# The down product placed behind the next expert's gate and up products, and the odd layer's stepped attention groups stored by residue

## The chip, the cores and the metric

The kernel runs on one core of a Trainium2 chip. The metric is device time in microseconds (us) of one execution of the whole program. The program is a static list of instructions for each engine: TensorE (PE; its weight loads are the row PEld), VectorE (DVE), ScalarE (ACT), GpSimd (POOL) and SyncE (SP), which issues most of the DMA transfers. Each engine works its own list in order and waits on semaphores for the others.

## The reference, cut to what matters

Three blocks follow one another on 512 tokens of width 1024. The first ends in a mixture of 16 experts, in which each expert takes the 64 tokens of highest affinity; the third holds an attention over three groups of keys, of which two are spaced.

```python
aff = softmax(h @ w_router)                # 512 tokens x 16 experts
g, idx = top_k(aff.T, 64)                  # each expert takes its 64 tokens
xin = h[idx]                               # 16 x 64 x 1024
a = xin @ w_gate[e];  u = xin @ w_up[e]    # weights 1024 x 1024 fp32 each
y = (silu(a) * u) @ w_down[e]
y = y * g                                  # then added back to the rows idx
...
DIL_CONFIGS = ((128, 1), (512, 4), (2048, 16))   # window and step of the three groups
# odd layer, one group: a query sees keys 0, dil, 2*dil, ... behind it
s = q @ k[:, local].T * scale - slope * steps;  s[not valid] = -inf
o = softmax over the three groups together, times v
```

## The kernel before, in words

**Weights.** All weights lie in device memory in the order in which they are used, in chunks of [128, 2048] fp32 (1 MB). `fetch` (L372) issues one transfer for a chunk from SP into a ring of buffers; in the expert stage the ring has seven buffers (two of the pool `wp`, five of `pc`), and a transfer waits until the chunk that had its buffer has been used. `pieces` takes a chunk as two pieces of [128, 1024] and writes each as a sum of two reduced-precision parts: ACT copies the high part (`whi`), DVE subtracts it and keeps the rest (`wlo`). PE multiplies with both. Piece 5 of each product (`WHOLE`) is not split: PE takes it from the raw chunk in full fp32, so that chunk's buffer comes free when PE has used it.

**Expert stage (`phase_b`).** Every engine call of the stage but POOL's and SP's is pinned to program order, through a wrapper, so that ACT, DVE and PE run the stage in the order of the Python code; in the profile nearly all of it carries the wrapper's line, L279, and tiles tell the operations apart. One product (`prod`) is eight pieces, "slots 0 to 7"; at each slot the code first draws the next pieces (`piece`, which keeps up to `ahead` pieces converted beyond the one in use, 2 at first and 5 after the first down product has opened the pool `pm`), then runs the side work that is hung on this slot (`hooks`), then issues the slot's matmuls.

`_moe_order` writes out the order of the products: gate and up of expert 0; then gate of e+1, down of e, up of e+1; at the end gate 15, up 15, down 14, down 15.

The side work consists of generators that are advanced one step at a time:

- `gather(e)`: an indirect DMA of the expert's 64 rows from POOL into `xn`, then two steps that transpose them on PE into a bank named `tp` and split them into `xs` (ACT high part, DVE rest); the second also copies one block in full fp32 to `xfull`.
- `activ(e)`: two steps, each of 16 matmul instructions on the gate result `ag` and the up result `xn`, then ACT's SiLU, DVE's product `sg`, and the split into `act`. The first step uses two `tp` banks, the second two `av` banks; there are two of each.
- `pair(p, n)`: the finished rows `yt` of two experts are scaled by DVE, a selection matrix `ph` is made, and the rows are split into `y`; n is 1 (all 1024 columns at once) but for the last pair.
- `scatter`: PE adds the rows of one or two pairs back by a matmul with `ph` into an `av` bank, DVE adds the bank to `x`; eight steps for each group of `GROUPS`.

After an up product ACT copies the result to `xn` (`first`); after a down product ACT copies halves to `ya` and DVE adds them into `yt` (`down`).

**Odd layer (`phase_e`).** `qk` makes `qz` and `kT` of a pair of heads (tokens along the free axis) by projecting, then copying from the result bank. `far` forms the scores of the two spaced groups for four residues c:

```python
nc.tensor.matmul(ps[:, sl], qz[:, t, c::4], kT[:, c::4], start=True, stop=True)
```

Both operands are read with a step of four fp32 elements. In this phase the framework orders instructions itself.

Of the kernel before, what the change touches and what calls it, by code (L numbers as in the profile page):

```python
# [52 lines left out]


def _moe_order():
    o = [("g", 0), ("u", 0)]
    for e in range(NE):
        if e + 1 < NE:
            o.append(("g", e + 1))
        o.append(("d", e))  # L60
        if e + 1 < NE:
            o.append(("u", e + 1))
    o[-3:] = [o[-2], o[-3], o[-1]]
    return o


# [225 lines left out]
class Kernel:  # L292
# [737 lines left out]
    def phase_b(self, er, ep, after):  # L1030
# [72 lines left out]
        def gather(e):  # L1103

            xg = self.nrm.tile([128, D], F32, name="xn", tag="xn")
            nc.gpsimd.indirect_dma_start(out=xg[:CAP], out_offset=None, in_=self.hd[:, :],
                                         in_offset=bass.IndirectOffsetOnAxis(ap=idxg[:, e:e + 1], axis=0))
            yield
            st = pw.tile([128, 8, 128], F32R, name="xs")
            xs[e] = st, xfull[:, e % 2]  # L1110
            for g in range(2):
                pt = self.tp()
                for k in range(4):
                    kk = 4 * g + k
                    nc.tensor.transpose(pt[:, k * CAP:(k + 1) * CAP], xg[:CAP, kk * 128:(kk + 1) * 128],
                                        self.ident[:CAP, :CAP])
                t = pt[:, :4 * CAP].rearrange("p (k c) -> p k c", k=4)
                self.split(st[:, 4 * g:4 * g + 4, :CAP], st[:, 4 * g:4 * g + 4, CAP:], t)
                for n, k in enumerate(WHOLE):
                    if k // 4 == g:  # L1120
                        nc.scalar.copy(xfull[:, e % 2, n, :CAP], t[:, k % 4])
                yield

        def prod(stat, full, hooks):
# [30 lines left out]
        def activ(e):  # L1155
            a = [asb.pop((t, e)) for t in "gu"]
            last = e + 1 == NE
            st = pw.tile([128, 8, 128], F32R, name="act", tag="xs" if last else "act", bufs=2 if last else 1)
            full = xfull[:, NE % 2] if last else afull
            act[e] = st, full  # L1160
            for g in range(2):
                pg, pu = (self.av(), self.av()) if g else (self.tp(), self.tp())
                for src, pt in zip(a, (pg, pu)):
                    for k in range(4):
                        f = 4 * g + k
                        nc.tensor.matmul(pt[:, k * 128:(k + 1) * 128], src[:, f * 128:(f + 1) * 128], dup,
                                         start=True, stop=True)
# [31 lines left out]

        iota = None  # L1200

        def pair(p, n):

            t = rows.pop(p)
            y = pm.tile([128, 2, D], F32R, name="y", bufs=3)
            ph = pm.tile([128, S], F32R, name="ph", bufs=3)
            ys[p] = y, ph
            for i in range(n):
                sl = slice(i * D // n, (i + 1) * D // n)
                nc.vector.scalar_tensor_tensor(t[:, sl], t[:, sl], gp[:, p:p + 1], self.g2[:, sl], op0=OP.mult, op1=OP.mult)  # L1210
                if i == 0:
                    nc.vector.tensor_scalar(ph, iota, idxp[:, p:p + 1], None, op0=OP.is_equal)
                    yield
                self.split(y[:, 0, sl], y[:, 1, sl], t[:, sl])
            yield

        def scatter(ps_, c):

# [19 lines left out]
        gath, acts = gather(0), none  # L1238
        for _ in range(3):
            next(gath)  # L1240
        scat = fin = none
        for t, e in order:
            if t == "g":
                gath = gather(e + 1) if e + 1 < NE else none
                first(t, e, {0: [gath], 2: [acts], 3: [acts], 5: [scat], 7: [scat]})
            elif t == "u":
                fresh = fin is not none
                first(t, e, {1: [fin], 2: [gath], 3: [none if fresh else scat], 4: [gath], 5: [fin],
                             7: [none if fresh else scat]})
                fin = none  # L1250
                acts = activ(e)
            else:
                down(e, {2: [acts], 3: [acts], 4: [scat], 5: [scat], 6: [scat], 7: [scat]} if e + 2 == NE else {})
                if e % 2:
                    p = e // 2
                    fin = pair(p, 2 if e + 1 == NE else 1)
                    if p in GROUPS:
                        list(scat)
                        scat = scatters(GROUPS[p]) if e + 1 < NE else none
        list(fin)  # L1260
        self.nc = nc = plain
        self.parts = []
        el.close()
# [260 lines left out]
    def phase_e(self, hT, after):  # L1524
        nc, tc, sp = self.nc, self.tc, self.sp
        with ExitStack() as es:
# [25 lines left out]
            def qk(scale=1.0):  # L1552
                qz = p.tile([128, 2, S], F32, name="qz", bufs=3)
                nc.gpsimd.memset(qz[64:, 0], 0.0)
                nc.gpsimd.memset(qz[:64, 1], 0.0)
                kT = p.tile([128, S], F32, name="kT", bufs=3)
                for t, w in enumerate(self.pieces("qk", 128)):
                    ps = self.mm()
                    self.proj_s(hT, w, ps)
                    if t == 0:  # L1560
                        nc.scalar.activation(qz[:64, 0], ps[:64], AF.Copy, scale=scale)
                        nc.vector.tensor_scalar(qz[64:, 1], ps[64:], scale, None, op0=OP.mult)
                    else:
                        nc.scalar.copy(kT, ps)
                return qz, kT

            def stick(pr):
# [56 lines left out]
            def dilated(pr):  # L1624
# [20 lines left out]
                def far(g, db, qz, kT):  # L1645
                    for t in range(2):
                        ps = self.mm()
                        for c in range(4):
                            sl = slice(c * 128, (c + 1) * 128)
                            nc.tensor.matmul(ps[:, sl], qz[:, t, c::4], kT[:, c::4], start=True, stop=True)  # L1650
                        for c in range(4):
                            sl = slice(c * 128, (c + 1) * 128)
                            nc.vector.tensor_tensor_reduce(s12[g - 1][t][:, c], ps[:, sl], db[:, t], 1.0, NEG,
# [204 lines left out]
```

## Time and profile before

| | us |
|---|---|
| median of 3 runs (2100.42 to 2102.78) | 2101.84 |
| the profiled execution, its own time | 2099.54 |
| span of the profiled execution | 2097.8 |

The span is what the trace covers; 1.7 us of the execution lie around it. The median of the runs is 2.3 us above the profiled execution's own time. Sums are made against the profiled execution.

The expert stage runs from about 280 to 826 us of the span, the odd layer from about 1480 to 1690 us.

### The profile page before, as it was taken

How to read it: one execution, taken by the hardware profiler on the slowest of the kernel's cores; microseconds unless marked ns; L12 is line 12 of the kernel's file. 1: busy time of each engine (PE TensorE's matmuls, PEld its weight loads, DVE VectorE, ACT ScalarE, POOL GpSimd, SP SyncE). 2: the span in 40 equal slices, each digit the busy share in tenths (PEclk: the TensorE clock that was granted, in tenths of full speed). 3: DMA queues.
4: the chain of work that ended last, by engine and by line, in shares of the span. 5: the costliest groups of instructions: out<-in, count | busy, mean ns of one | idle time of the engine just before them, and what ended most of it. 6: DMA issues, size and time to landing. Idle time of an engine off the chain costs nothing.

```text
span 2097.8 us, 24799 instructions
## 1 busy us (share of the span) xinstructions
PE 1966.8 (94%) x9203; PEld 1554.2 (74%) x9203; DVE 1362.1 (65%) x2286; ACT 1060.8 (51%) x1835; POOL 153.3 (7%) x146
## 2 busy tenths in 40 slices
PE   5889869999999998999989999999999989999998
PEld 5667746767677676877778888888887768888886
DVE  7776478898988888627766533554537676534653
ACT  3335358777777876436544433443325554423432
POOL 2003500000000001000110000001100010000001
PEclk9889979999999999999999999999999999999999
DMA  7653648998999995220123222221421023222221
GB/s 292 195 170 125 285 175 338 366 384 354 405 383 366 389 396 209 91 91 11 61 81 108 94 91 101 101 88 64 133 71 61 33 79 121 96 96 100 81 96 56
DMA packets 53933, 358.30 MB, mean 171 GB/s; under 512 B 6694, under 2 KB 7262, under 8 KB 14004
## 3 DMA queue, kind: packets, MB, share of 16 engines
q1 hardware_dynamic: 48148, 338.60, 42.5%
q0 software_dynamic: 5664, 18.12, 3.2%
q8 instruction: 72, 1.18, 0.2%
q14 instruction: 49, 0.40, 0.1%
HBM read 353.28 MB, written 4.46 MB: 171 GB/s over the span
## 4 chain that ended last, share of the span: by engine, by line
PE 76%; DVE 10%; issue 6%; ACT 5%; DMA 3%; POOL 0%; SPq 0%; ACTq 0%; DVEq 0%; POOLq 0%
PE mm L279 13%; PE mm L411 13%; PE mm L412 13%; PE mm L413 13%; DVE wlo L279 3%; PE av L279 2%; PE av L413 2%; PE av L412 2%; PE av L411 2%; PE tp L411 2%; PE tp L413 2%; ACT whi L279 2%; PE tp L412 2%; DMA wraw<-in_wts 2%; PE mm L1289 1%
## 5 line engine op out<-in xcount | busy, mean ns | idle before, releaser
L402 DVE TENSOR_TENSOR wlo<-wraw,whi 128x1024 fp32r<-128x1024 f32 (+2 forms) x209 | 250.6, 1201 | 412.2 <-ACT whi L401 412.1
L279 DVE TENSOR_TENSOR wlo<-wraw,whi 128x1024 fp32r<-128x1024 f32 x336 | 393.9, 1219 | 46.1 <-ACT whi L279 44.3
L401 ACT CAST whi<-wraw 128x1024 fp32r<-128x1024 f32 (+2 forms) x209 | 214.8, 1030 | 356.5 <-PE mm L412 145.3
L411 PE MATMUL mm<-hT_hi,whi 128*128 128x512 f32 (+1 forms) x960 | 375.3, 392 | 5.1 <-ACT whi L401 4.9
L412 PE MATMUL mm<-hT_lo,whi 128*128 128x512 f32 (+1 forms) x960 | 374.1, 390 | 0.4 <-DVE hT_lo L417 0.4
L413 PE MATMUL mm<-hT_hi,wlo 128*128 128x512 f32 (+1 forms) x960 | 373.8, 390 | 0.0
L279 ACT CAST whi<-wraw 128x1024 fp32r<-128x1024 f32 x336 | 333.1, 1050 | 15.8 <-PE mm L279 14.8
L411 PEld LDWEIGHTS mm<-hT_hi,whi 128*128 128x128 f32 x960 | 182.3, 190 | 46.3 <-ACT whi L401 5.7
L412 PEld LDWEIGHTS mm<-hT_lo,whi 128*128 128x128 f32 x960 | 182.3, 190 | 41.2 <-DVE hT_lo L417 1.6
L413 PEld LDWEIGHTS mm<-hT_hi,wlo 128*128 128x128 f32 x960 | 182.3, 190 | 39.8
L279 PE MATMUL mm<-whi,xs 128*128 128x512 f32 x448 | 199.7, 446 | 2.3 <-ACT whi L279 2.3
L279 PE MATMUL mm<-wlo,xs 128*128 128x512 f32 x448 | 183.1, 409 | 4.0 <-DVE wlo L279 3.7
L279 PEld LDWEIGHTS mm<-wlo,xs 128*128 128x128 f32 x448 | 86.6, 193 | 36.5 <-DVE wlo L279 14.5
L412 PE MATMUL mm<-wlo,hT_hi 128*128 128x512 f32 (+2 forms) x288 | 110.8, 385 | 1.1 <-DVE wlo L402 1.1
L411 PE MATMUL mm<-whi,hT_hi 128*128 128x512 f32 (+2 forms) x288 | 110.9, 387 | 0.0
L413 PE MATMUL mm<-whi,hT_lo 128*128 128x512 f32 (+2 forms) x288 | 110.2, 384 | 0.6 <-DVE hT_lo L417 0.6
L279 PEld LDWEIGHTS mm<-whi,xs 128*128 128x128 f32 x448 | 86.8, 194 | 27.3 <-issue 6.2
L279 PE MATMUL mm<-whi,act 128*128 128x512 f32 x224 | 94.4, 422 | 0.0
L279 PE MATMUL mm<-wlo,act 128*128 128x512 f32 x224 | 89.3, 399 | 0.5 <-DVE wlo L279 0.5
L416 ACT CAST aT_hi<-cv 128x512 fp32r<-128x512 f32 x44 | 27.3, 621 | 117.0 <-DVE cv L1767 117.0
L1766 ACT ACTIVATE cv<-cv 128x512 f32<-128x512 f32 x44 | 27.8, 632 | 89.2 <-DVE cv L1763 89.2
L411 PE MATMUL tp<-whi,aT_hi 128*128 128x512 f32 x176 | 69.4, 395 | 0.0
(502 smaller groups left out, 3382.5 us busy)
## 6 DMA issues: line engine op xcount, KB each, us to landing
wraw<-in_wts SPq DMA_DIRECT2D x310, 1024.0 KB, 7.6
wraw<-in_wts SPq DMA_DIRECT2D x8, 768.0 KB, 4.2
x<-in_x SPq DMA_DIRECT2D x4, 512.0 KB, 11.5
out<-x SPq DMA_DIRECT2D x4, 512.0 KB, 2.6
wraw<-in_wts SPq DMA_DIRECT2D x2, 832.0 KB, 4.5
bias<-t5scr POOLq DMA_DIRECT2D x8, 192.0 KB, 15.2
hd<-xn POOLq DMA_DIRECT2D x3, 512.0 KB, 3.3
mod<-md POOLq DMA_DIRECT2D x1, 1024.0 KB, 11.1
```

The source lines that it names most:

```text
L279: ins = op(*a, **k)
L401: i1 = nc.scalar.copy(hi[:, :n], t[:, a:a + n])
L402: i2 = nc.vector.tensor_tensor(lo[:, :n], t[:, a:a + n], hi[:, :n].bitcast(F32), op=OP.subtract)
L411: mm(ps, a[0], b[0], start=start, stop=False)
L412: mm(ps, a[0], b[1], start=False, stop=False)
L413: mm(ps, a[1], b[0], start=False, stop=stop)
L416: self.nc.scalar.copy(hi, src)
L1289: nc.tensor.matmul(ps[:, :W], lhs[:, i * 128:(i + 1) * 128], rhs[:, :W], start=True, stop=True)
L1766: nc.scalar.activation(u[0], u[0], AF.Silu)
```

## The change

Three things change in the expert stage and one in the odd layer.

- The order becomes gate e+1, up e+1, down e for every expert; the special order at the end falls away, as it now comes out by itself.
- The side work is hung on other slots. Both halves of `activ` use `tp` banks and stand at slots 4 and 6 of the next gate product (slots 2 and 3 before; slots 1 and 3 of down 14 for the last expert). The gather's DMA for expert e+2 is issued at slot 0 of a down product instead of slot 0 of a gate product (for the first experts as before); its transposes stay at slots 2 and 4 of the up product before. `pair` always works in four steps of half the width and is chained with the scatters into one generator `work`, which is advanced at slots 1 and 7 of a gate product, 1 and 6 of an up product, 2 and 5 of a down product.
- In `gather`, the copy to `xfull` is issued before the split instead of behind it.
- In the odd layer, `qk(residue=True)` stores `qz` and `kT` of the two spaced groups with the four residues one behind the other: the copies out of the result bank read with a step of four, and `far` reads contiguous slices.

```diff
 def _moe_order():
     o = [("g", 0), ("u", 0)]
     for e in range(NE):
         if e + 1 < NE:
-            o.append(("g", e + 1))
+            o += [("g", e + 1), ("u", e + 1)]
         o.append(("d", e))
-        if e + 1 < NE:
-            o.append(("u", e + 1))
-    o[-3:] = [o[-2], o[-3], o[-1]]
     return o
...
-                self.split(st[:, 4 * g:4 * g + 4, :CAP], st[:, 4 * g:4 * g + 4, CAP:], t)
                 for n, k in enumerate(WHOLE):
                     if k // 4 == g:
                         nc.scalar.copy(xfull[:, e % 2, n, :CAP], t[:, k % 4])
+                self.split(st[:, 4 * g:4 * g + 4, :CAP], st[:, 4 * g:4 * g + 4, CAP:], t)
...
-                pg, pu = (self.av(), self.av()) if g else (self.tp(), self.tp())
+                pg, pu = self.tp(), self.tp()
...
-        def pair(p, n):
+        def pair(p):
...
-            for i in range(n):
-                sl = slice(i * D // n, (i + 1) * D // n)
+            for half in range(2):
+                sl = slice(half * 512, half * 512 + 512)
                 nc.vector.scalar_tensor_tensor(t[:, sl], t[:, sl], gp[:, p:p + 1], self.g2[:, sl], op0=OP.mult, op1=OP.mult)
-                if i == 0:
+                yield
+                self.split(y[:, 0, sl], y[:, 1, sl], t[:, sl])
+                yield
+                if half == 0:
                     nc.vector.tensor_scalar(ph, iota, idxp[:, p:p + 1], None, op0=OP.is_equal)
-                    yield
-                self.split(y[:, 0, sl], y[:, 1, sl], t[:, sl])
-            yield
...
             if t == "g":
-                gath = gather(e + 1) if e + 1 < NE else none
-                first(t, e, {0: [gath], 2: [acts], 3: [acts], 5: [scat], 7: [scat]})
+                hooks = {0: [gath] if e < 2 else [], 4: [acts], 6: [acts]}
+                for k in (1, 3, 5, 7) if e + 1 == NE else (1, 7):
+                    hooks[k] = [work]
+                first(t, e, hooks)
             elif t == "u":
-                fresh = fin is not none
-                first(t, e, {1: [fin], 2: [gath], 3: [none if fresh else scat], 4: [gath], 5: [fin],
-                             7: [none if fresh else scat]})
+                hooks = {2: [gath], 4: [gath]}
+                for k in (1, 3, 5, 6, 7) if e + 1 == NE else (1, 6):
+                    hooks[k] = [work]
+                first(t, e, hooks)
                 acts = activ(e)
-            else:
-                down(e, {2: [acts], 3: [acts], 4: [scat], 5: [scat], 6: [scat], 7: [scat]} if e + 2 == NE else {})
+                gath = gather(e + 2) if e + 2 < NE else none
+            elif e + 1 < NE:
+                hooks = {0: [gath], 2: [work], 5: [work]}
+                if e + 2 == NE:
+                    hooks = {1: [acts], 3: [acts], 2: [work], 4: [work], 5: [work], 6: [work], 7: [work]}
+                down(e, hooks)
...
+            def qk(scale=1.0, residue=False):
+                order = lambda t: t.rearrange("p (a c) -> p c a", c=4) if residue else t
+                place = lambda t: t.rearrange("p (c a) -> p c a", c=4) if residue else t
...
-                        nc.scalar.copy(kT, ps)
+                        nc.scalar.copy(place(kT), order(ps))
...
-                            nc.tensor.matmul(ps[:, sl], qz[:, t, c::4], kT[:, c::4], start=True, stop=True)
+                            nc.tensor.matmul(ps[:, sl], qz[:, t, sl], kT[:, sl], start=True, stop=True)
...
-                o1 = qk()
+                o1 = qk(residue=True)
...
-                o2 = qk()
+                o2 = qk(residue=True)
```

## Rows read from the trace of the kernel before

**Rows 1.** The page's busy times: us, share of the span, instructions.

```profile
PE 1966.8 (94%) x9203; PEld 1554.2 (74%) x9203; DVE 1362.1 (65%) x2286; ACT 1060.8 (51%) x1835; POOL 153.3 (7%) x146
```

**Rows 2.** Windows of four experts, last to stage end: busy times, PEclk, DMA share, GB/s.

```profile
321.80:457.72 135.92, 126.64 (x553) 92.16 (x552) 119.92 (x127) 105.28 (x145) 6.21 (x4) 0.97 0.97 379
457.72:593.18 135.46, 129.34 (x578) 97.16 (x577) 121.15 (x131) 104.11 (x143) 6.79 (x4) 0.97 0.96 380
593.18:727.42 134.24, 128.13 (x578) 95.73 (x577) 119.92 (x130) 103.62 (x142) 7.77 (x4) 0.99 0.96 376
727.42:826.00 98.58, 94.22 (x421) 70.68 (x419) 87.80 (x98) 70.37 (x97) 8.86 (x9) 0.98 0.86 339
```

**Rows 3.** Windows of one expert, from down product to down product (slot 5).

```profile
321.80:354.29 32.49, 30.79 (x138) 21.86 (x137) 27.56 (x30) 25.27 (x35) 2.50 (x1) 1.00 0.99 380
...
526.24:555.67 29.43, 29.43 (x138) 22.04 (x136) 25.63 (x28) 23.26 (x33) 3.40 (x1) 1.00 1.01 406
555.67:593.18 37.51, 33.83 (x146) 24.91 (x145) 33.93 (x37) 28.64 (x40) 0.89 (x1) 0.95 0.99 395
593.18:626.28 33.10, 33.10 (x154) 25.14 (x153) 29.74 (x34) 25.66 (x36) 1.31 (x1) 1.00 0.96 381
626.28:661.81 35.53, 33.07 (x145) 25.10 (x144) 31.96 (x35) 26.54 (x37) 1.22 (x1) 0.95 0.94 370
```

**Rows 4.** PE's timeline around one gate product: start, length, operation, [idle before].

```profile
571.95 1.06 PE L279 MATMUL tp<-c_dup,ag 128*128 128x128 f32 x8
575.99 1.16 PE L279 MATMUL tp<-c_dup,xn 128*128 128x128 f32 x8 [2.98 <-ACT xn L279]
...
578.51 1.91 PE L279 MATMUL av<-c_dup,ag 128*128 128x128 f32 x8
```

**Rows 5.** ACT's timeline just before that.

```profile
571.46 0.21 ACT L279 COPY xfull<-tp 128x64 f32<-128x64 f32 x1 [4.99 <-DVE xs L279]
...
572.52 1.04 ACT L279 CAST y<-yt 128x1024 fp32r<-128x1024 f32 x1
...
575.35 1.07 ACT L279 COPY xn<-mm 128x512 f32<-128x512 f32 x2
```

**Rows 6.** DVE's timeline in the up product before.

```profile
563.01 1.30 DVE L279 TENSOR_TENSOR yt<-mm,ya 64x512 f32<-64x512 f32 x2
...
565.56 1.27 DVE L279 SCALAR_TENSOR_TENSOR yt<-yt,gp,row_g 128x1024 f32<-128x1024 f32 x1
...
571.01 0.42 DVE L279 TENSOR_TENSOR xs<-tp,xs 128x256 fp32r<-128x256 f32 x1
```

**Rows 7.** Waits from 400 to 800 us: who for whom, total us, times, longest.

```profile
ACT xfull L279 <- DVE xs L279: 46.6, 12, 5.3
ACT act L279 <- DVE sg L279: 35.0, 24, 1.7
DVE wlo L279 <- ACT whi L279: 30.0, 39, 1.2
...
PE tp L279 <- ACT xn L279: 16.9, 7, 3.0
DVE act L279 <- ACT act L279: 11.3, 24, 0.5
```

**Rows 8.** PE's timeline in the odd layer: spaced-group scores, then the contiguous group's.

```profile
1555.64 7.62 PE L1650 MATMUL mm<-kT,qz 128*128 128x128 f32 x32
1563.08 0.56 PE L1615 MATMUL tp<-pm_parts,perm 128*128 128x6 bf16 x16
...
1606.57 2.33 PE L1640 MATMUL mm<-kT,qz 128*128 128x128 f32 x12
1608.74 0.49 PE L1707 MATMUL tp<-ident,s 128*128 128x128 f32 x3
```

**Rows 9.** Instructions of single lines of the odd layer: ns least, median, most.

```profile
L1653 DVE CUSTOM_DVE_ANT_0 s<-mm,dil x32: 285/286/292, 1557.9 to 1638.2; 128x128 f32<-128x128 f32 x32
...
L1564 ACT COPY kT<-mm x8: 566/578/580, 1530.3 to 1653.6; 128x512 f32<-128x512 f32 x8
```

More of the change, by code (lines that the diff above doesn't have):

```diff
@@ L1237, in phase_b @@
         none = iter(())
[L1238 to L1241, printed above, removed]
+        gath, acts, work = gather(0), none, none
+        list(itertools.islice(gath, 3))
+        gath = gather(1)
         for t, e in order:
             if t == "g":
-                gath = gather(e + 1) if e + 1 < NE else none
-                first(t, e, {0: [gath], 2: [acts], 3: [acts], 5: [scat], 7: [scat]})
+                hooks = {0: [gath] if e < 2 else [], 4: [acts], 6: [acts]}
+                for k in (1, 3, 5, 7) if e + 1 == NE else (1, 7):
+                    hooks[k] = [work]
+                first(t, e, hooks)
             elif t == "u":
-                fresh = fin is not none
-                first(t, e, {1: [fin], 2: [gath], 3: [none if fresh else scat], 4: [gath], 5: [fin],
-                             7: [none if fresh else scat]})
-                fin = none
+                hooks = {2: [gath], 4: [gath]}
+                for k in (1, 3, 5, 6, 7) if e + 1 == NE else (1, 6):
+                    hooks[k] = [work]
+                first(t, e, hooks)
                 acts = activ(e)
-            else:
-                down(e, {2: [acts], 3: [acts], 4: [scat], 5: [scat], 6: [scat], 7: [scat]} if e + 2 == NE else {})
+                gath = gather(e + 2) if e + 2 < NE else none
[4 more added lines that the diff above has]
+                down(e, hooks)
                 if e % 2:
                     p = e // 2
-                    fin = pair(p, 2 if e + 1 == NE else 1)
                     if p in GROUPS:
-                        list(scat)
-                        scat = scatters(GROUPS[p]) if e + 1 < NE else none
-        list(fin)
+                        list(work)
+                        work = itertools.chain(pair(p), scatters(GROUPS[p]))
+                    else:
+                        work = itertools.chain(pair(p), work)
+            else:
+                down(e, {})
+                list(work)
+                list(pair(e // 2))
         self.nc = nc = plain
@@ L1550, in value @@
                 self.proj_m(hT, "v", 2, 8, 512, evac, residue=t == 1)
-            def qk(scale=1.0):
+            def qk(scale=1.0, residue=False):
+                order = lambda t: t.rearrange("p (a c) -> p c a", c=4) if residue else t
+                place = lambda t: t.rearrange("p (c a) -> p c a", c=4) if residue else t
                 qz = p.tile([128, 2, S], F32, name="qz", bufs=3)
@@ L1560, in qk @@
                     if t == 0:
-                        nc.scalar.activation(qz[:64, 0], ps[:64], AF.Copy, scale=scale)
-                        nc.vector.tensor_scalar(qz[64:, 1], ps[64:], scale, None, op0=OP.mult)
+                        nc.scalar.activation(place(qz[:64, 0]), order(ps[:64]), AF.Copy, scale=scale)
+                        nc.vector.tensor_scalar(place(qz[64:, 1]), order(ps[64:]), scale, None, op0=OP.mult)
                     else:
-                        nc.scalar.copy(kT, ps)
+                        nc.scalar.copy(place(kT), order(ps))
                 return qz, kT
```

## The prediction

> **What bounds the kernel now.** I read the page's busy times first: PE is busy 94% of the span [rows 1], but that is an average over stages. The change touches two: the expert stage (some 545 us) and the odd layer (some 210 us).
>
> For the expert stage I cut the trace into windows from the fp32 matmuls (slot 5) of one down product to those of another. Three stretches of four experts take 135.92, 135.46 and 134.24 us, 405.6 us for twelve experts or 33.80 us each [rows 2]. In none of them is one engine full: of 135.46 us DVE is busy 121.15, and the DMA share is 0.96. So I look for what each would need alone, and for what stops them.
>
> *PE.* The window 526.24 to 555.67 has no scatter step and no stall; PE is busy all its 29.43 us. The window 593.18 to 626.28 has four scatter steps of a two-pair group and takes 33.10, again without a gap: (33.10 - 29.43) / 4 = 0.92 us a step [rows 3]. Four experts hold eight such steps (two pairs), so PE needs 4 x 29.43 + 8 x 0.92 = 125.1 us, 31.3 an expert. The other 10 of 135 us are stalls.
>
> *The stalls* lie in the expert whose rows complete a pair: 37.51 us with two scatter steps (29.43 + 1.84 = 31.3 without a stall, so 6.2 lost) and 35.53, also with two (4.2 lost); both windows show a mean granted clock of 0.95 [rows 3]. The chain there, read backwards: PE waits 2.98 us at 575.99 for ACT's copy of the up result `xn`, which `activ` needs, and then runs at the lower clock level for a while: 8 instructions on `ag` take 1.91 us where 1.06 was normal [rows 4]. ACT made that copy late because it had stood 4.99 us before the tiny `xfull` copy, waiting for DVE's `xs`, and had then to make a full-width `y` [rows 5]. DVE was late because the down product's `yt` and the pair's full-width step, 1.30 + 1.27 us and a selection matrix, fell together into one up product [rows 6]. Over 400 us the wait before `xfull` is the longest of ACT's list (46.6 us in 12 times), and PE's for `xn` is 16.9 us in 7 [rows 7].
>
> *DMA.* 380 GB/s x 135.46 us / 4 = 12.87 MB an expert. At the rate of the three stretches, brought to a share of 1 (379/0.97, 380/0.96, 376/0.96: about 393 GB/s) [rows 2], an expert needs 32.7 us.
>
> *DVE.* 121.15 / 4 = 30.3 us of work [rows 2], and waits that the new order keeps: for ACT's `act`, 11.3 us over the 11.8 experts of 400 us, 1.0 each; for `whi`, 30.0 us or 2.5 each, of which about 1.2 follows the `xfull` wait and goes [rows 7]. That is 32.6.
>
> So behind the stalls stands a limit of 32.6 to 32.7 us an expert, by DMA and DVE alike, and PE's 31.3 below it.
>
> **Term 1, the experts in steady state.** Removed is the coincidence: `xn` of expert e+1 is now read at slot 4 of gate e+2, and a whole down product and four slots lie between, twelve slots where it was two; a slot is 29.43 / 24 = 1.2 us in the window without stalls [rows 3]. The `xfull` copy goes ahead of the split, so ACT no longer waits for DVE there; DVE's `xs` waits instead for one more ACT copy of 0.21 us [rows 5], nothing against 5. The pair's work comes as four steps over a gate and an up product. In the up product after a pair, DVE had 1.30 + 1.27 + 0.5 + 1.2 us on top of its pieces; now at most two half steps of 0.6 to 1.1. Half-width steps cost next to nothing more: two instructions of 512 columns take DVE 1.30 us, one of 1024 takes 1.27 [rows 6]. I take 32.7: 12 x (33.80 - 32.7) = -13.2 us. Bounds: DMA held at the weakest full window (380 GB/s at 0.99, 33.5 us): -3.6; PE alone, 31.3: -30.
>
> Weighed against a page: here one core runs, and windows of one expert reach 406 GB/s at a share of 1.01 [rows 3]. The Trainium skill, "HBM Reference", Specifications, gives about 358 GB/s as a core's effective share and about 425 for a core that streams alone. By 358 an expert would need 35.9 us, more than it takes already, so the trace refutes it; by 425 it would need 30.3, PE would set the pace, and the term would be -30.
>
> **Term 2, the start.** The deeper look-ahead (5 pieces) starts with the first down product, which now comes one product later. The expert in which it starts lost 32.49 - 29.43 = 3.1 us [rows 3]; that loss stays, and one more product runs with look-ahead 2. I take half of it, +1.5 (bounds 0 and +3.1). The selection constant's load moves with the pool; it is first needed an expert later.
>
> **Term 3, the end of the stage** (727.42 to 826, 98.58 us). It holds one more pair stall of the same form; the DMA share is 0.86 there, so DMA does not take its place [rows 2]. I price it at the mean of the two above: -5.2. `activ` of expert 15 moves from slots 2 and 3 to 1 and 3, one slot (1.2 us) nearer to its `xn` copy; the ACT copy takes 1.07 [rows 5] and slot 1's `ag` instructions come first: 0, bound +1. The last pair was already split in two halves: 0.
>
> **Moved at no cost.** The gather's indirect DMA goes from a gate product's slot 0 to a down product's; POOL's queue holds nothing else, its transposes come one gate product and more later, and the buffer it waits for is free since the transposes of the gather before. The weight transfers keep number and size, only their order in memory follows the products. Both halves of `activ` now use the two `tp` banks: the second half, two slots (2.5 us) behind, must wait until SiLU and DVE's `sg` have read the first; ACT waits 35.0 / 24 = 1.5 us for `sg` as it is [rows 7], so I price this at 0 as long as DVE lags by less than that slack (rival D).
>
> **Term 4, the odd layer.** The 32 instructions of 128 columns on stepped operands take 1563.08 - 1555.64 = 7.44 us, 0.2325 each. The contiguous group's first 12 instructions hold 20 blocks of 128 columns (widths 128 and 256) in 1608.74 - 1606.57 = 2.17 us, 0.1085 a block [rows 8]. So 32 x 0.124 = 4.0 us fewer, twice: -7.9. PE has no gap before, in or behind them, and projections of the next unit follow, so I count it whole but for DVE, which takes up the banks: 0.285 us each at most [rows 9], 1.1 us for the four of a bank beside PE's new 0.87; the excess of about 1 us lies under the projections that PE runs before the next result is needed. The result copies now read in steps of four. No row shows such a copy: from below 0 extra; from above the factor of the stepped matmuls, 2.1, so 0.64 us more on the 0.578 of ACT's `kT` [rows 9], and as much for `qz`. Copies are off PE's list and the first spaced group's matmuls (1.7 us) cover the second's copies: nearest to 0. I take -7.5 (bounds -8 and -4).
>
> [...]
>
> **Sum.** -13.2 + 1.5 - 5.2 - 7.5 = -24.4 us: 2099.54 - 24.4 = 2075.1 for the profiled execution; with the 2.3 us by which the median stands above it, 2077.4.
>
> **Rivals.**
> - B, PE sets the pace: twelve experts at 31.3, so -30 + 1.5 - 5.2 - 7.5 = -41.2: 2060.6. For it: the window at 406 GB/s; against it: the 393 of whole stretches.
> - C, DMA is as good as full already and the stalls were time in which it caught up: 33.5 an expert, -3.6 + 1.5 - 5.2 - 7.5 = -14.8: 2087. For it: shares of 0.99 to 1.01 in three of the five windows. Against it: 0.94 to 0.97 over whole stretches.
> - D, slower: PE waits at slot 6 of each gate product for `sg` to free the banks that `activ` used at slot 4. It decides from 24.4 / 16 = 1.5 us an expert on; with DVE as late as the 4.99 us that ACT saw, less 2.5 of slack and 1.1 in which `ag` goes first [rows 4], it is 1.4, and a fallen clock as above doubles it: 16 x 2.8 - 24.4 = +20: 2122. For it: DVE is the fullest engine beside PE. Against it: the late moments were those of bunched pair work, which is spread.
> - E, the stage does not gain: DVE's lag only moves from the up product after a pair into gate and up alike, and PE waits for `wlo` as long in all. Then the odd layer alone remains: 1.5 - 7.5 = -6: 2096.
> - F, stepped copies are so slow that the odd layer gains nothing: 2085.
>
> **Chances.** Forecast 0.50 (its own range 2068 to 2083), B 0.13, C 0.18, D 0.06, E 0.08, F 0.05. A measurement of this kernel tells 0.2% (4.2 us) from no change. Faster than 2097.6: all but D and a part of E, 0.88; within: 0.06; slower: 0.06. The range takes in B and C and leaves out D, most of E and a little beyond B: 2059 to 2092.
>
> **What the profile after would show.** Right: PE's waits for `xn` and ACT's for `xfull` gone; no fall of the granted clock in mid-stage; twelve experts in about 392 us with a DMA share near 1; L1650 at about 0.11 us an instruction, its weight loads as short as those of L1640. Wrong: `tp` matmuls waiting for `sg` (D); windows of 33.5 us with ACT waiting for `wraw` (C); PE waiting for `wlo` in gate products (E); copies of `kT` above 1.2 us with PE waiting for them (F).

## The result and the profile after

The changed kernel takes 2075.61 us (median of 4 runs, 2071.76 to 2079.41) beside 2101.13 for the kernel before in the same comparison (2098.72 to 2102.78): a ratio of 0.9882, 95% interval 0.9863 to 0.9902. The prediction was 2077. The profiled execution takes 2075.10, its span 2073.3, so 24.4 us less than the profiled execution of before, against a predicted sum of 24.4.

That the sum fits so well is partly luck. The experiments below show that one exchanged pair of statements brings more than the whole gain in the expert stage, and that the new order of the products, with the slots, banks and half-width steps that go with it, costs time, although the prediction gave the gain to that order.

Busy times of the page after (compare [rows 1]):

```profile
PE 1953.7 (94%) x9203; PEld 1537.2 (74%) x9203; DVE 1359.7 (66%) x2300; ACT 1060.1 (51%) x1842; POOL 149.5 (7%) x146
```

Windows of four experts after, and the rest of the stage (columns as in [rows 2]: stretch, length, busy PE, PEld, DVE, ACT, POOL, granted clock, DMA share, GB/s):

```profile
331.94:461.75 129.81, 123.73 (x554) 89.06 (x553) 117.37 (x128) 105.58 (x147) 4.89 (x4) 1.00 1.00 396
461.75:593.57 131.82, 128.10 (x578) 94.03 (x577) 121.11 (x135) 103.16 (x145) 5.65 (x4) 1.00 0.99 395
593.57:725.63 132.06, 128.42 (x578) 93.93 (x577) 121.23 (x135) 103.32 (x144) 6.66 (x6) 1.00 0.98 385
725.63:818.00 92.37, 84.27 (x381) 62.85 (x379) 83.65 (x98) 63.56 (x87) 8.95 (x9) 1.00 0.82 321
```

Twelve experts take 393.69 us where they took 405.62, 32.8 each, and the granted clock no longer falls. Windows of one expert after (compare [rows 3]):

```profile
528.82:559.10 30.28, 29.87 (x137) 22.08 (x136) 27.46 (x30) 24.13 (x35) 1.55 (x1) 1.00 1.00 399
559.10:593.57 34.47, 32.39 (x146) 23.44 (x145) 31.64 (x36) 28.27 (x40) 0.90 (x1) 1.00 1.01 405
593.57:629.17 35.60, 35.25 (x161) 26.75 (x160) 33.38 (x39) 26.46 (x37) 1.42 (x1) 1.00 0.95 376
629.17:660.65 31.48, 30.59 (x138) 21.75 (x136) 28.64 (x33) 24.30 (x36) 1.79 (x1) 1.00 0.95 367
```

The two slow experts of before (37.51 and 35.53) have become 34.47 and 31.48, but the windows don't hold the same work: 35.60 has six scatter steps where 33.10 had four, and 31.48 has none where 35.53 had two. By the prediction's own measure (29.43 us, and 0.92 for each scatter step) the four windows after stand 0.9, 3.2, 0.7 and 2.1 us above a length without stalls, some 6.8 us in all; before it was 10.4, all of it in two windows. So the long stalls have shrunk, and each of the two windows that had none has a small one.

Waits from 400 to 800 us after (compare [rows 7]: engine and tile that wait, for whom, total us, times, longest):

```profile
ACT act L277 <- DVE sg L277: 64.0, 25, 4.6
DVE wlo L277 <- ACT whi L277: 20.5, 34, 0.7
...
DVE act L277 <- ACT act L277: 11.8, 25, 0.5
...
PE tp L277 <- DVE sg L277: 6.7, 9, 1.5
ACT whi L277 <- DMA wraw<-in_wts: 4.8, 9, 1.0
PE mm L277 <- DVE wlo L277: 3.4, 10, 0.5
```

ACT's 46.6 us before `xfull` and PE's 16.9 before `xn` are gone. ACT now stands 64.0 us before `act` (35.0 before), and PE waits 6.7 us for `sg` in a place where it did not wait. What matters most below is the second line: DVE's wait for `whi` has gone from 30.0 to 20.5.

The odd layer after: PE's timeline of one unit of spaced scores (compare [rows 8]),

```profile
1540.89 3.73 PE L1660 MATMUL mm<-kT,qz 128*128 128x128 f32 x32
1544.46 0.54 PE L1625 MATMUL tp<-pm_parts,perm 128*128 128x6 bf16 x16
```

and single lines (operation, count, ns least / median / most, first and last start; compare [rows 9]), the kernel before first:

```profile
L1650 PEld LDWEIGHTS mm<-kT,qz x64: 308/330/330, 1555.4 to 1636.9; 128*128 128x128 f32 x64
L1650 PE MATMUL mm<-kT,qz x64: 396/414/414, 1555.6 to 1637.1; 128*128 128x128 f32 x64
L1561 ACT ACTIVATE qz<-mm x8: 574/584/587, 1524.7 to 1653.1; 64x512 f32<-64x512 f32 x8
L1562 DVE TENSOR_SCALAR qz<-mm x8: 695/695/696, 1526.1 to 1653.9; 64x512 f32<-64x512 f32 x8
```

and after:

```profile
L1660 PEld LDWEIGHTS mm<-kT,qz x64: 188/192/193, 1540.7 to 1614.6; 128*128 128x128 f32 x64
L1660 PE MATMUL mm<-kT,qz x64: 271/275/276, 1540.9 to 1614.7; 128*128 128x128 f32 x64
L1571 ACT ACTIVATE qz<-mm x8: 575/582/587, 1509.9 to 1630.5; 64x512 f32<-64x512 f32 x8
L1572 DVE TENSOR_SCALAR qz<-mm x8: 694/694/695, 1511.3 to 1631.3; 64x512 f32<-64x512 f32 x8
L1574 ACT COPY kT<-mm x8: 567/578/582, 1515.5 to 1631.0; 128x512 f32<-128x512 f32 x8
```

The 32 instructions take 1544.46 - 1540.89 = 3.57 us where they took 7.44. The same 64 weight loads were 330 ns in the median before, and the matmuls 414. Half of the copies now read the result bank with a step of four, and least, median and most are within 2 ns of what they were.

### The profile page after: what moved, and what is told of

It reads as the page before. It is cut to its first block, busy times and chain, and to the rows that moved or that the text cites. A ratio compares the mean times of both kernels' runs of the same rounds, so it can differ in the third digit from the quotient of the medians.

```text
span 2073.3 us, 24795 instructions
## 1 busy us (share of the span) xinstructions
PE 1953.7 (94%) x9203; PEld 1537.2 (74%) x9203; DVE 1359.7 (66%) x2300; ACT 1060.1 (51%) x1842; POOL 149.5 (7%) x146
## 4 chain that ended last, share of the span: by engine, by line
PE 52%; issue 4%; DVE 3%; ACT 1%; POOL 0%; DMA 0%; DVEq 0%; POOLq 0%; ACTq 0%
PE mm L409 12%; PE mm L410 12%; PE mm L411 12%; PE av L410 2%; PE av L411 2%; PE av L409 2%; PE tp L409 2%; PE tp L411 2%; PE tp L410 2%; PE mm L1296 1%; PE av L1450 1%; PE tp L1313 1%; DVE xn L474 0%; DVE wlo L400 0%; ACT junk L440 0%
## 5 line engine op out<-in xcount | busy, mean ns | idle before, releaser
L277 DVE TENSOR_TENSOR wlo<-wraw,whi 128x1024 fp32r<-128x1024 f32 x336 | 394.9, 1220 | 35.2 <-ACT whi L277 34.3
L277 PE MATMUL mm<-whi,xs 128*128 128x512 f32 x448 | 189.7, 424 | 1.7 <-ACT whi L277 1.7
L277 PEld LDWEIGHTS mm<-whi,xs 128*128 128x128 f32 x448 | 85.5, 191 | 23.2 <-ACT whi L277 3.8
```

What stands on the lines that cost most here:

```text
L277: ins = op(*a, **k)
```

## The experiments

A comparison of medians can't tell 2 us apart here, and the stage begins anywhere from 274.6 to 283.3 us in these traces though no kernel differs ahead of it. So beside the median I read three lengths in each trace: the expert stage from the first to the last matmul of its products; the twelve experts between the same marks as above; and the first and last eight products, from the fp32 matmuls (slot 5) of the first of the eight to those of the eighth. These stretches overlap (the first and the last eight reach into the twelve experts), so their differences don't add up to the stage's. Medians of the kernel before in the four comparisons were 2098.4, 2097.4, 2094.3 and 2098.1.

| kernel | us | ratio, 95% | stage | twelve | first 8 | last 8 |
|---|---|---|---|---|---|---|
| before | | | 544.30 | 405.61 | 74.70 | 83.86 |
| after | 2075.61 | 0.9882 [0.9863, 0.9902] | 534.62 | 393.69 | 75.79 | 84.69 |
| odd_only | 2089.55 | 0.9963 [0.9950, 0.9975] | 543.55 | 405.41 | 74.73 | 83.85 |
| before_xfull_first | 2076.68 | 0.9897 [0.9882, 0.9911] | 526.20 | 389.93 | 72.94 | 81.04 |
| after_xfull_behind | 2096.94 | 0.9996 [0.9987, 1.0004] | 555.16 | 412.52 | 77.22 | 86.62 |
| after_tail | 2074.35 | 0.9886 [0.9872, 0.9901] | 535.22 | 393.52 | 75.82 | 85.91 |
| best | 2069.07 | 0.9868 [0.9851, 0.9885] | 523.72 | 388.26 | 72.95 | 80.99 |
| after_early_pool | 2073.65 | 0.9886 [0.9869, 0.9902] | 532.85 | 392.28 | 74.58 | 84.70 |
| after_av_half | 2080.72 | 0.9912 [0.9896, 0.9927] | 536.77 | 395.23 | 75.81 | 86.13 |
| probe_dma | 2084.26 (one run) | | 541.52 | 400.34 | 75.82 | 85.25 |
| probe_dve | 2087.35 (one run) | | 546.47 | 401.82 | | |
| probe_pe | 2072.65 (one run) | | 537.06 | 395.14 | | |
| no_gather | 2074.69 (one run) | | 534.23 | 393.57 | | |
| best_split_later | 2053.68 | 0.9796 [0.9781, 0.9812] | 511.01 | 378.83 | 72.63 | 77.96 |

### The parts one by one

**odd_only** is the kernel before with the odd layer's part of the change alone.

```diff
-    nc.tensor.matmul(ps[:, sl], qz[:, t, c::4], kT[:, c::4], start=True, stop=True)
+    nc.tensor.matmul(ps[:, sl], qz[:, t, sl], kT[:, sl], start=True, stop=True)
...
-                o1 = qk()
+                o1 = qk(residue=True)
```

> The kernel before with the odd layer's part alone. Theory (the stepped matmuls were on PE's path and the copies read in steps for nothing): 64 instructions drop from 0.2325 to about 0.11 us, 7.7 us less, so about 2093.5 us against 2101 for the kernel before. Rival (the odd layer takes more than its matmuls, as the trace after seems to show 9.6 us between the start and the end of that layer): 2091.5. Rival (given back at later waits): 2097 or more.

8.9 us faster with an untouched expert stage (543.55 beside 544.30), between the 7.7 of the theory and the 9.6 of the first rival. Term 4 stands.

**before_xfull_first** is the kernel before with one exchange: in `gather`, the copy to `xfull` ahead of the split. **after_xfull_behind** is the changed kernel with that exchange undone (the same lines the other way round).

```diff
-                self.split(st[:, 4 * g:4 * g + 4, :CAP], st[:, 4 * g:4 * g + 4, CAP:], t)
                 for n, k in enumerate(WHOLE):
                     if k // 4 == g:
                         nc.scalar.copy(xfull[:, e % 2, n, :CAP], t[:, k % 4])
+                self.split(st[:, 4 * g:4 * g + 4, :CAP], st[:, 4 * g:4 * g + 4, CAP:], t)
```

> The kernel before with the one swap of the xfull copy and the split. Theory (two causes together: ACT held before xfull, and DVE late through bunched pair work): ACT's wait goes, PE's wait for xn shrinks from 3 us to under 1, but DVE stays late and PE waits for wlo or sg instead: twelve experts in about 399 us instead of 405.6, the whole about 2095. Rival (the swap alone is the gain): twelve experts in about 394 us, the whole about 2089. Rival (nothing: DVE's lag alone sets it): 405 and 2101.

> The changed kernel with the xfull copy back behind the split. Theory (a whole down product now lies between the up product's copy and its use, so a late ACT costs nothing): twelve experts within 2 us of 393.7, the whole 2075 to 2078. Rival (the swap is what freed ACT and is the main gain): ACT waits 3 to 5 us an expert again, twelve experts 400 or more, the whole 2083 to 2088.

Both runs went beyond the forecasts made for them: before_xfull_first takes 2076.68 us, and 389.93 for the twelve experts, where at best 2089 and 394 were expected; after_xfull_behind takes 2096.94 where at worst 2088 was. The exchange is worth more than any of them allowed.

The four kernels make a square. In the order of before, the exchange shortens the stage from 544.30 to 526.20, by 18.1 us; in the order of the change from 555.16 to 534.62, by 20.5. The new order with all that goes with it makes the stage 10.9 us longer without the exchange and 8.4 longer with it; which part of it (order, slots, banks, half-width steps) costs this was tested for the banks and for the steps at the end alone. Waits from 400 to 800 us in before_xfull_first,

```profile
ACT act L279 <- DVE sg L279: 55.1, 26, 4.5
...
DVE wlo L279 <- ACT whi L279: 18.2, 32, 0.7
```

and in after_xfull_behind:

```profile
ACT act L277 <- DVE sg L277: 68.0, 24, 5.2
DVE wlo L277 <- ACT whi L277: 34.3, 50, 1.2
ACT xfull L277 <- DVE xs L277: 28.9, 11, 3.1
```

In the kernel before, PE's wait for `xn` [rows 4] goes with the exchange alone: no such line stands in this stretch of before_xfull_first. With the new order and the old place of the copy ACT still waits 28.9 us for `xs`, and DVE's wait for `whi` is the longest of the four kernels, 34.3 us. PE's longest wait there is one for `sg` (12.7 us), and none for `xn` is left. Since the exchange gains as much in this order, its gain does not hang on PE's wait for `xn`.

**after_tail** spreads the pair's and scatters' steps of the last experts as in other experts, and hangs what is left on the last down product.

```diff
-                for k in (1, 3, 5, 7) if e + 1 == NE else (1, 7):
+                for k in (1, 7):
...
-                for k in (1, 3, 5, 6, 7) if e + 1 == NE else (1, 6):
+                for k in (1, 6):
...
-                down(e, {})
+                down(e, {1: [work], 3: [work], 5: [work], 6: [work]})
                 list(work)
```

> The changed kernel with the side work of the last experts hung as on all others, at two slots a product, and the rest of it at slots 1, 3, 5 and 6 of down 15. Theory (the predicted 5 us at the end of the stage did not come because four steps of the pair were put into gate 15, where DVE and ACT are late with them and PE waits for y and x): the time from down 12 to the last product falls by 4 to 5 us, the whole to about 2071. Rival (the end is held by DVE's or the transfers' lag, wherever the steps hang): no change, 2075.

The stage stays at 535.22 and the last eight products take 85.91 instead of 84.69. That the bunching of these steps costs the end its gain is refuted.

**after_early_pool** opens the deeper look-ahead behind the fourth product of the stage, as before the change; `deeper` holds the lines that `down` had under `if pm is None`.

```diff
                 first(t, e, hooks)
+                if e == 1:
+                    deeper()
                 acts = activ(e)
```

> The changed kernel with the deeper look-ahead (and the pool that it needs) opened behind the second up product, the fourth product of the stage as in the kernel before, instead of behind the first down product, now the fifth. Theory (term 2): the stage's start loses by running one more product with a look-ahead of 2, so 1.5 to 3 us come back: 2073, stage 532 to 533. Rival: the start is set by DMA from the first product on and the look-ahead does not matter: 2075.6, stage 534.6.

The first eight products give back 1.2 us, the stage 1.8: the expected size, though the median can't tell it from no change.

**after_av_half** gives the second half of `activ` its own banks again.

```diff
-                pg, pu = self.tp(), self.tp()
+                pg, pu = (self.av(), self.av()) if g else (self.tp(), self.tp())
```

> The changed kernel with the second half of the SwiGLU step again in the two av banks, as before the change. Theory (rival D in small): the matmuls on ag and xn wait 6.7 us in 400 for sg to free the tp banks; with other banks these waits go, and if they are paid at the end 16 x 0.5 = up to 8 us of the stage come back: 2068 to 2072. Rival: a wait there only lets transfers catch up, which set the pace: 2075.6 within 1.5.

Both expectations missed: the waits on `tp` are gone from PE's list (6.7 us to none), but the stage gets 2.2 us longer. PE waits elsewhere instead:

```profile
PE mm L277 <- DVE wlo L277: 8.3, 19, 0.8
...
PE av L277 <- ACT sg L277: 3.7, 3, 1.4
```

**best** joins the exchange and the odd layer's part on the kernel before; order, hooks, banks and pair are those of before.

```diff
+ the lines of before_xfull_first
+ the lines of odd_only
```

> The kernel before with the exchanged pair of statements (xfull copy ahead of the split) and with the odd layer by residue; product order, hooks, banks and pair steps of before. If the exchange is what the expert stage gains and the two parts add: 2098.4 - 21.8 - 8.9 = about 2068, some 7 us under the changed kernel, with an expert stage of 526 us. Rival: the shorter odd layer and the shorter stage share a gain (the tail of the stage loads for what follows): 2073 or more.

2069.07 and a stage of 523.72: the two parts add. This version lies 6.5 us under the changed kernel by the medians; the intervals of the ratios overlap (0.9868 beside 0.9882), but the stages differ by 10.9 us.

### What sets the pace

Four probes on the changed kernel, each putting work on one resource or taking it off.

```diff
 probe_dma:  two loads more at slot 0 of each up product
+    nc.sync.dma_start(dummy, <256 KB of wts>)
 probe_dve:  two operations more at slot 0 of each up product
+    nc.vector.tensor_tensor(dummy, dummy, dummy, op=OP.mult)
 probe_pe:   four matmuls more at slot 1 of each up product
+    nc.tensor.matmul(ps[half], stat[:, 1], w[0][:, 0, sl], start=False, stop=False)
 no_gather:  experts 2 to 15
-    nc.gpsimd.indirect_dma_start(out=xg[:CAP], ...)
+    nc.gpsimd.memset(xg[:CAP], 0.5)
```

> The changed kernel with two loads of 256 KB more per expert (0.52 MB beside its 12.87), of data that nothing reads. If transfers set the pace of the steady experts (32.8 us): 0.52 MB at 393 GB/s is 1.33 us an expert, 16 us over the twelve, 34.1 an expert. If VectorE sets it: under 0.3 us an expert. If both bind by turns: about half, 0.7.

> The changed kernel with two VectorE products of 128x512 fp32 more per expert, on a scratch tile, at slot 0 of each up product. If VectorE is a limit of the steady experts (30.3 us of work and the waits between): about 2 x 0.6 = 1.2 to 1.3 us an expert, 15 us over the twelve. If the order of the products costs through late wlo pieces, the same or more. If transfers set the pace: under 0.3 us an expert.

> The changed kernel with four more matmuls of 512 columns in each up product, at slot 1; the up result counts one block three times by it, so the output is another. If TensorE sets the pace: 4 x 0.23 = 0.9 us an expert, 11 us over the twelve. If it has the slack that the prediction gave it (31.3 of 32.8 us): under 0.3 us an expert.

> The changed kernel with the token rows of experts 2 to 15 not gathered: a constant is written in their place, so the output is another. The gather is a POOL transfer in 4 KB rows beside the weight stream. If transfers set the pace: its 0.26 MB are 0.7 us an expert, 8 us over the twelve, 32.1 an expert. If VectorE or TensorE does: under 0.3 us.

- probe_dve: 401.82 - 393.69 = 8.1 us, 0.68 an expert, for two operations of 688 ns, so 1.38 us of work. Half of it is paid, between the two forecasts (1.2 and under 0.3).
- probe_dma: 6.7 us, 0.55 an expert. Its first four experts take 129.82 us, as without the loads (129.81); then 134.56 and 135.96, so 0.7 and 1.0 an expert where 1.33 was expected of a full bound. ACT's wait for `wraw` rises from 4.8 to 21.6 us.
- probe_pe: 1.45 us, 0.12 an expert for four matmuls (0.9 expected of a bound).
- no_gather: 0.12 us less in all, where 8 were expected if transfers set the pace. The last two windows of four experts:

```profile
460.61:592.46 131.85, 128.10 (x578) 93.91 (x577) 121.14 (x135) 103.38 (x145) 3.81 (x4) 1.00 0.96 382
592.46:724.32 131.86, 128.07 (x577) 93.89 (x576) 121.13 (x135) 103.21 (x145) 10.18 (x6) 1.00 0.97 386
```

Fewer transfers gain nothing and only lower the share (0.96 and 0.97 where it was 0.99 and 0.98), more transfers cost up to 1.0 us an expert: transfers do not set the changed kernel's pace, though they have little to spare. PE has most of the slack that the prediction gave it. DVE pays half of what is added to it, and its waits for ACT say where the other half went (work added to ACT was not tried). DVE's balance in the last window of four experts, work plus the two waits (`wlo` for `whi`, `act` for `act`), beside the window's length:

| kernel | DVE busy | waits for ACT | sum | window |
|---|---|---|---|---|
| before | 119.92 | 10.0 + 3.8 | 133.7 | 134.24 |
| after | 121.23 | 6.7 + 3.8 | 131.7 | 132.06 |
| probe_dve | 125.94 | 4.8 + 3.8 | 134.5 | 134.81 |
| best | 120.44 | 4.8 + 3.8 | 129.0 | 129.27 |

DVE's and PE's waits in this window of after:

```profile
DVE wlo L277 <- ACT whi L277: 6.7, 11, 0.7
DVE act L277 <- ACT act L277: 3.8, 8, 0.5
PE tp L277 <- DVE sg L277: 2.1, 3, 1.3
PE mm L277 <- DVE wlo L277: 1.4, 4, 0.5
```

and best's window and its waits:

```profile
577.88:707.15 129.27, 125.97 (x577) 94.28 (x576) 120.44 (x131) 104.11 (x143) 6.08 (x4) 1.00 1.01 397
DVE wlo L279 <- ACT whi L279: 4.8, 8, 0.7
DVE act L279 <- ACT act L279: 3.8, 8, 0.5
PE av L279 <- ACT sg L279: 2.9, 2, 1.8
PE mm L279 <- DVE wlo L279: 0.4, 1, 0.4
```

But for 0.3 to 0.5 us, DVE is idle for no other reason. In probe_dve 4.7 us of work come on top, the waits for `whi` shrink by 1.9, and the window grows by 2.75. The exchange takes 5.2 us from DVE's waits in this window, and the window is 5.0 shorter (before to best). After and best differ by 0.8 us of DVE work and 1.9 of waits, together 2.7 of the 2.8 by which the window is longer.

The sum alone does not name the engine that sets the pace. PE's work and waits fill the window as well: 128.42 + 2.1 + 1.4 = 131.9 of 132.06 in after. What sets the two apart is the probes (half of the added DVE work is paid, an eighth of the added PE work) and after_av_half (PE's wait for `sg` taken away, nothing gained). That DVE, held up by ACT, sets most of the pace is argued from these; no run takes work from DVE alone.

The waits themselves are seen in the changed kernel. ACT's timeline (start, length, operation, [idle before]):

```profile
568.35 0.37 ACT L277 ACTIVATE sg<-tp 128x256 f32<-128x256 f32 x1
573.34 0.41 ACT L277 CAST act<-sg 128x256 fp32r<-128x256 f32 x1 [4.62 <-DVE sg L277]
573.65 1.99 ACT L277 CAST whi<-wraw 128x1024 fp32r<-128x1024 f32 x2
```

and DVE's:

```profile
569.36 3.49 DVE L277 TENSOR_TENSOR wlo<-wraw,whi 128x1024 fp32r<-128x1024 f32 x3
572.88 0.42 DVE L277 TENSOR_TENSOR sg<-sg,tp 128x256 f32<-128x256 f32 x1
573.78 0.43 DVE L277 TENSOR_TENSOR act<-sg,act 128x256 fp32r<-128x256 f32 x1 [0.47 <-ACT act L277]
574.72 2.36 DVE L277 TENSOR_TENSOR wlo<-wraw,whi 128x1024 fp32r<-128x1024 f32 x2 [0.52 <-ACT whi L277]
```

ACT has its SiLU done at 568.7 and stands 4.62 us, because the split into `act` is next on its list and DVE still has three `wlo` ahead of `sg`. The `whi` of the next pieces stand behind `act`. So when DVE has made `sg`, it waits 0.47 for `act`'s high part and then 0.52 for a `whi` that ACT could have made in those 4.62 us. Twice an expert, this is about 1 us each time.

**best_split_later** puts the split one slot behind the product, so that one piece's `whi` and `wlo` lie between.

```diff
-                sg = pw.tile([128, 4, CAP], F32, name="sg", bufs=1)
+                sg = pw.tile([128, 4, CAP], F32, name="sg", bufs=2)
...
                 nc.vector.tensor_tensor(sg, sg, pu..., op=OP.mult)
+                yield
                 self.split(st[:, 4 * g:4 * g + 4, :CAP], st[:, 4 * g:4 * g + 4, CAP:], sg)
                 for n, k in enumerate(WHOLE):
                     if k // 4 == g:
                         nc.scalar.copy(full[:, n, :CAP], sg[:, k % 4])
-                yield
...
-                first(t, e, {0: [gath], 2: [acts], 3: [acts], 5: [scat], 7: [scat]})
+                first(t, e, {0: [gath], 2: [acts], 3: [acts], 4: [acts], 5: [scat], 7: [scat]})
...
-                down(e, {2: [acts], 3: [acts], 4: [scat], 5: [scat], 6: [scat], 7: [scat]} if e + 2 == NE else {})
+                down(e, {2: [acts], 3: [acts], 4: [acts, scat], 5: [scat], 6: [scat], 7: [scat]} if e + 2 == NE else {})
```

> The kernel before with the exchange and the odd layer by residue, and now the split of each SwiGLU half one slot behind the product that it splits (a second sg buffer; three steps at slots 2, 3 and 4). Theory: VectorE's work and its waits for ScalarE set the pace together (119.4 to 120.4 busy and 8.6 waiting of 129.3 us for four experts); the waits come from ScalarE standing before act until VectorE has made sg, so whi of the next piece comes late. Without them VectorE needs 30.1 us an expert and TensorE, at 31.3, becomes the bound: 1.0 us an expert and 12 to 15 us in all, 2054 to 2058. Rival: transfers at a share of 1.00 and 395 GB/s hold the same 32.3 us: 2069 within 2, with ScalarE waiting for wraw instead.

2053.68 us, 15.4 under best, and 2.0% under the kernel before; the stage is 12.7 us shorter than in best. That is 0.3 us under the forecast of 2054 to 2058, and the rival (2069) is out. Windows of four experts:

```profile
317.59:442.23 124.64, 121.46 (x554) 89.74 (x553) 118.52 (x127) 107.03 (x144) 6.00 (x4) 1.00 1.01 400
442.23:568.83 126.60, 125.58 (x578) 94.33 (x577) 120.52 (x131) 105.59 (x142) 11.26 (x4) 1.00 1.01 406
568.83:696.42 127.59, 126.44 (x577) 94.25 (x576) 120.57 (x131) 105.71 (x142) 11.71 (x4) 1.00 1.01 407
```

PE is busy 125.58 of 126.60 and 126.44 of 127.59 us, 31.6 us an expert over the twelve: now it is close to the bound that the prediction worked out for it, 31.3. DVE's timeline around one SwiGLU step:

```profile
495.62 0.41 DVE L279 TENSOR_TENSOR sg<-sg,tp 128x256 f32<-128x256 f32 x1
495.95 1.22 DVE L279 TENSOR_TENSOR wlo<-wraw,whi 128x1024 fp32r<-128x1024 f32 x1
497.08 0.42 DVE L279 TENSOR_TENSOR act<-sg,act 128x256 fp32r<-128x256 f32 x1
497.42 0.42 DVE L279 TENSOR_TENSOR sg<-sg,av 128x256 f32<-128x256 f32 x1
497.75 1.22 DVE L279 TENSOR_TENSOR wlo<-wraw,whi 128x1024 fp32r<-128x1024 f32 x1
```

No idle time stands before any of them. In the last window DVE's wait for `act` is gone (3.8 us in best); for `whi` 6.1 are left. From 400 to 800 us ACT waits 12.9 us for `sg`, in best 54.9. Transfers run at 406 and 407 GB/s, and ACT's waits for `wraw` rise from 6.9 us in best to 23.2: transfers may come to their bound together with PE; no run here separates the two. PE's own wait for ACT's `sg`, 8.9 us in best, is 1.7 here, so the gain can't be given to DVE's waits alone: both shrink when ACT stands less before `act`.

## Why the prediction was right, and where it was not

**What bounds the kernel.** The limit of 32.6 to 32.7 us an expert held (32.8 measured), and it was right for DVE: 30.3 us of work, 1.0 for `act`, and 1.3 forecast for `whi`, which came out as 6.7 / 4 = 1.7. For DMA it was wrong: 393 GB/s was the rate that the kernel asked for, not a ceiling, as 407 in best_split_later shows. A share near 1 did not tell the two apart; taking transfers away did (no_gather). Nor was the limit a floor: best takes 32.4 us an expert and best_split_later 31.6, since DVE's waits, counted in it as kept, could be taken away.

**Term 1** (-13.2, measured -11.9) is right in size and wrong in its cause. The stall was read as a chain from bunched pair work through `xs` and `xfull` to a late `xn`, and the cure was said to be the distance of twelve slots and the spreading; the exchange stood between them without a price of its own. It is the other way round. The exchange alone gives -15.7 for the twelve experts, the order and spread steps without it +6.9. ACT's wait of 46.6 us was not slack: behind `xfull` stood the `whi` pieces for which DVE, with no idle time but such waits, then waited. The prediction had the rows for it: it counted about 1.2 us an expert of `whi` waits as following the `xfull` wait, and of the four-expert window the exchange takes 5.2 us of DVE's waits, 1.3 an expert.

"Half-width steps cost next to nothing more" was judged by a row of two instructions; on an engine with as little idle time as DVE it counts. `yt` and `y` of a pair in halves take 4 x 742 + 4 x 684 = 5.7 us in four experts, at full width, as best shows, 2 x 1281 + 2 x 1216 = 5.0.

**Term 2** (+1.5): the first eight products take 1.1 us more than before; 1.2 come back when the look-ahead opens a product earlier. The size is right; the difference is too small for the medians to show.

**Term 3** (-5.2) did not come. The last eight products take 0.8 us more than before. The exchange alone brings -2.8 there, so a pair stall did go; the new order takes back 3.7. Neither the steps' places (after_tail) nor the opening of the pool changes that, and other banks make it longer. What exactly is late there was not settled: from down 12 to the end PE waits 4.0 us in the trace after (1.6 for `x`, 1.8 for `y`) and 2.2 in before_xfull_first, too little alone, and in after_tail, where the waits for `y` are gone, the end is no shorter. So the stall was priced too high (2.8 by the exchange, where 5.2 was put), and a cost of 3.7 that the new order brings to the end was put at nothing; where that cost comes from stays open.

**Term 4** (-7.5): 2 x (7.44 - 3.57) = -7.7 on PE's list, and odd_only is 8.9 faster (interval 5.2 to 10.5). The copies in steps of four out of the result bank cost nothing; their bound of +0.64 us each did not come near. The Trainium skill, "SBUF — State Buffer", "Door 1: The DMA port swizzle" (note on cachelines), says that any non-contiguous access pattern in PSUM, the memory of the result banks, slows matmuls significantly. Of copies out of it the note says nothing, and here they take as long with the step as without (ACT 582 ns with the step in half of them, 584 without; DVE 694 and 695).

**The sum** fits because misses cancel. The stage was to become 16.9 us shorter (-13.2 + 1.5 - 5.2) and became 9.7 shorter; of the 7.2 that are missing, most is term 3's. Against that the stage begins 1.6 us earlier (281.0 before, 279.4 after), and what lies behind its last matmul is 13.2 us shorter (1272.4 and 1259.3 us), 5.6 more than the 7.5 of term 4. The 1.6 us are within what the start of the stage varies by. Of the 5.6, 2.1 us lie between the last product and the next layer's first transposition (16.66 us before, 14.61 after), where the last scatter's 16 matmuls run without a break, and 1.8 in the odd layer itself, which from its first to its last instruction on PE takes 149.9 us before and 140.6 after (142.0 in odd_only), 9.3 less where 7.5 was put. No run isolates either, and for the rest no cause was found. A sum right to a tenth is luck.

**The rivals.** D's wait came in small (6.7 us in 400, at most 1.5 each), and removing it gained nothing, as PE then waited elsewhere (8.3 us for `wlo`, 3.7 for ACT's `sg`). C forecast 33.5 us an expert, 32.8 came, and no_gather speaks against its mechanism. B, the pace of PE, is not what the change reached, but what best_split_later came near: 31.6 an expert beside the 31.3 worked out. E holds for the order: without the exchange the change measures 2096.94, where E forecast 2096, and its stage is longer than before. That the change landed in the forecast's range hung on the exchanged pair of statements.

## What to carry to other kernels

Rank waits by the engine on which added work costs time, not by their length or by the engine where they show: here 46.6 us of ACT's waits mattered because DVE's `whi` stood behind them, 6.7 us of PE's did not. For a candidate add its busy time and its own waits in one window: where the sum is the window's length, its list names all that holds it up. That is only a candidate, since two engines can both fill the window (DVE 131.7 and PE 131.9 of 132.06); a probe that adds work to one of them tells them apart. On engines that run a fixed list in order, an operation that waits for another engine belongs behind work that is already free to run: moving two statements and one `yield`, with a second `sg` buffer, gave 2.0% together with the shorter odd layer, where the whole change, which has the exchange and the odd layer in it too, gave 1.2%.

## What the runs showed of the hardware that was not expected

- Copies by ACT and DVE that read a result bank with a step of four fp32 elements take as long as contiguous ones (582 and 584 ns, 694 and 695 ns), while PE, with a step of four fp32 elements in both operands, took 330 ns for a weight load instead of 192 and 414 for a matmul instead of 275.
- A DMA share of 0.98 to 1.01 stood beside 385, 396 and 407 GB/s on one core, and a share of 0.99 and 0.98 fell to 0.96 and 0.97 without a gain when the gathers were left out: here a share near 1 did not mark a ceiling.
- ACT's copy to `xfull` waited for DVE's `xs` although both only read the same bank. With the copy first, ACT's wait is gone and DVE's has not appeared in its place. No run shows whether the wait is the chip's or one that the program sets between two readers of a bank.
